# Two transformer blocks on one core: the norms' per-token factors are worked out in PSUM, and those of q and kv are issued between the convolution's last two products

## The chip, the cores and the metric

The kernel runs on one core of a Trainium2 chip, in one launch. A core has five engines that work side by side, each through its own queue in order: PE (TensorE, matrix products and transposes into PSUM), DVE (VectorE), ACT (ScalarE), POOL (GpSimd) and SP, which here only issues transfers. [...] The time of a run is device microseconds from the first to the last instruction and what lies around them; a kernel is told by the median of its runs.

## The reference, cut to what matters

Two blocks work on a sequence of 512 tokens of width 1024. The first has a mixer of latent attention beside a gated causal convolution of width 31, a feed-forward net and a gate; the second another mixer, two squared-ReLU nets and a sparse attention. Norms stand ahead of nearly every part. The stage that the change moves work in is this one:

```python
def rms_norm(x, g):
    xf = x.astype(jnp.float32)
    y = xf * lax.rsqrt(jnp.mean(xf * xf, axis=-1, keepdims=True) + NORM_EPS)
    return (y * g.astype(jnp.float32)).astype(x.dtype)

    proj = xn @ w_in
    q_a, kv_a, k_rope, conv_in = jnp.split(proj, [o1, o2, o3], axis=-1)
    q = (rms_norm(q_a, g_q_a) @ w_q_b).reshape(...)
    kv = (rms_norm(kv_a, g_kv_a) @ w_kv_b).reshape(...)
    ...
    a, gate = jnp.split(conv_in, 2, axis=-1)
    c = a * jax.nn.sigmoid(gate)
    c = causal_depthwise_conv(c, conv_w, conv_b)
```

`q_a` is 384 wide, `kv_a` 256, `a` and `gate` 512 each; the first `rms_norm` of the block is applied late, as a factor per token.

## The kernel before

All activations stand transposed, 128 features by 512 tokens a tile. A product in fp32 is three products of split operands (high by high, high by low, low by high, lines 305 to 307), so each weight and each activation is split: ACT writes the high part (`whi`, line 280), DVE the rest (`wlo`, line 281). Raw weights land in two buffers `raw`, so the transfer of a weight unit waits until the `wlo` of the unit two before it has been made.

A norm needs one factor per token. `SumSq.add` squares the tiles and adds them up; `SumSq.rstd` lets PE sum over the features by products with a column of ones into four columns of a PSUM bank `t`, then works on 128x4 numbers: a scaled mean square `mv` in SBUF (line 439; with a factor `scale` lines 442 to 444), POOL's power of -1/2 into `y` (line 446), and one Newton step on DVE (lines 448 to 452, with a scale 454) that ends in `r`. There are 17 such calls, four of them with a scale: those of kv and of q, whose scale is the block's first norm factor `r1`, and two later. `row_tile` then has PE transpose the broadcast factor (line 462, `t<-ident,r`), and ACT copy it to SBUF as `R` (line 467).

The first mixer computes the convolution's four channel tiles in `conv_in(c)`: two weight units, gate product `pg` and value product `pa`, a sigmoid between, the padded tile `cp`. Each tile has 30 further taps: of even tiles ACT scales (`tap`, line 604) and POOL adds (`cy`, line 605), of odd tiles DVE does both (line 607). The tiles 0 to 2 come first, then kv's two units and `w_kr`, q's three units, and `conv_in(3)`. After that stands the copy of the rotated keys (`kr` by `rep`, line 674), then kv's `sk.rstd(r1)` and its rows `Fk`, q's `sq_.rstd(r1)` and its rows `Fq`. Next is the value product (lines 697 to 699), whose PSUM banks belong to a new phase of the pool: the first waits until ACT has read the last rows out of their bank. Line 765 makes the first key tile `kf`, with which the attention starts; it wants all 30 additions of tile 2 only after its last head.

The order on each engine is not written out by hand: the program is handed to a scheduler that simulates it and emits each engine's queue by its own estimate, with the taps at a high priority. A small edit therefore moves instructions in many places.

Of the kernel before, what the change touches and what calls it, by code (L numbers as in the profile page):

```python
# [7 lines left out]
FT = mybir.dt.float32  # L8
FR = mybir.dt.float32r
I32 = mybir.dt.int32  # L10
OP = mybir.AluOpType
# [11 lines left out]
EPS = 1e-6  # L23
# [191 lines left out]
def _body(tc, A, out):  # L215
    nc = tc.nc
    V, S, P, G = nc.vector, nc.scalar, nc.tensor, nc.gpsimd
# [3 lines left out]
    sp = tc.alloc_tile_pool(name="sp", bufs=2, reuse_waits="tile")  # L221
# [23 lines left out]
    def bank(tag):  # L245
        return ps[0].tile([128, T], FT, name=tag, bufs=banks[tag])
# [12 lines left out]
    def col(name, i):  # L259
        c = _COL0[name] + i  # L260
        return cols[:, c:c + 1]
# [3 lines left out]
    def unit(src, gain=None, eng=V, pl=None, size=1024, bufs=(2, 2), dst=None, chunks=1):  # L265

        n = src.shape[-1]
        pl = pl or wp
        raw = pl.tile([128, size], FT, name="raw", bufs=bufs[0])[:, :n]
        for i in range(chunks):  # L270
            a = slice(i * n // chunks, (i + 1) * n // chunks)
            nc.sync.dma_start(raw[:, a], src[:, a])
        if gain is not None:
            r3 = raw.rearrange("p (k c) -> p k c", k=KT)
            c0 = _COL0[gain]
            G.tensor_tensor(r3, r3, cols[:, c0:c0 + KT, None].to_broadcast([128, KT, n // KT]), op=OP.mult)
        hi, lo = dst or (pl.tile([128, size], FR, name=w, bufs=bufs[1])[:, :n] for w in ("whi", "wlo"))
        for i in range(chunks):
            a = slice(i * n // chunks, (i + 1) * n // chunks)
            S.copy(hi[:, a], raw[:, a])  # L280
            eng.tensor_tensor(lo[:, a], raw[:, a], hi[:, a], op=OP.subtract)  # L281
        return hi, lo

    def split(src, h, l, scale=None, eng=None):
        if scale is None:
            S.copy(h, src)  # L286
            (eng or V).tensor_tensor(l, src, h, op=OP.subtract)  # L287
        else:
            S.activation(h, src, AF.Copy, scale=scale)
            V.scalar_tensor_tensor(l, src, scale, h, op0=OP.mult, op1=OP.subtract)  # L290
        return h, l

    def split_in(pl, tag, src, scale=None, bufs=None, eng=None):
        h = pl.tile([128, T], FR, name=tag + "h", bufs=bufs)
        l = pl.tile([128, T], FR, name=tag + "l", bufs=bufs)
        return split(src, h, l, scale, eng)

    def mm(acc, u, acts, m=128, c0=0, cols_=128, first=True, last=True, ts=None):
        hi, lo = u
        n = len(acts)  # L300
        if ts is not None:
            acc, acts = acc[:, ts], [(h[:, ts], l[:, ts]) for h, l in acts]
        for k, (h, l) in enumerate(acts):
            s = slice(k * cols_ + c0, k * cols_ + c0 + m)
            P.matmul(acc, hi[:, s], h, start=first and k == 0, stop=False)  # L305
            P.matmul(acc, hi[:, s], l, start=False, stop=False)  # L306
            P.matmul(acc, lo[:, s], h, start=False, stop=last and k == n - 1)  # L307
# [6 lines left out]
    def gemm(src, acts, u=None, tag="mm"):  # L314
        acc = bank(tag)
        mm(acc, u or unit(src), acts)
        return acc
# [84 lines left out]
    class SumSq:  # L402
# [25 lines left out]
        def rstd(self, scale=None, ts=ALL):  # L428

            p = bank("t")  # L430
            b0, n = ts.start // 128, (ts.stop - ts.start) // 128
            for i in range(n):
                b = b0 + i
                tiles = [self.sum] if self.whole else [self.sum, self.last[b // 2]]
                for j, a in enumerate(tiles):
                    P.matmul(p[:, i:i + 1], a[:, b * 128:(b + 1) * 128], ones, start=j == 0, stop=a is tiles[-1])
            mv = sp.tile([128, 4], FT, name="mv")[:, :n]
            if scale is None:
                V.tensor_scalar(mv, p[:, :n], 1.0 / (128 * self.n), EPS, op0=OP.mult, op1=OP.add)
            else:  # L440
                scale = scale[:, b0:b0 + n]
                V.scalar_tensor_tensor(mv, p[:, :n], 1.0 / (128 * self.n), scale, op0=OP.mult, op1=OP.mult)
                V.tensor_tensor(mv, mv, scale, op=OP.mult)
                V.tensor_scalar(mv, mv, EPS, None, op0=OP.add)
            y = sp.tile([128, 4], FT, name="y")[:, :n]
            G.tensor_tensor(y, mv, mhalf[:, :n], op=OP.pow)
            a = sp.tile([128, 4], FT, name="a")[:, :n]
            V.tensor_tensor(a, mv, y, op=OP.mult)
            V.tensor_tensor(a, a, y, op=OP.mult)
            V.tensor_scalar(a, a, -0.5, 1.5, op0=OP.mult, op1=OP.add)  # L450
            r = sp.tile([128, 4], FT, name="r", bufs=4)[:, :n]
            V.tensor_tensor(r, y, a, op=OP.mult)
            if scale is not None:
                V.tensor_tensor(r, r, scale, op=OP.mult)
            return r

    def rows(c, p=None, ts=ALL):
# [7 lines left out]
    def row_tile(c, square=False):  # L465
        r = sp.tile([128, T], FT, name="R", bufs=2)
        S.activation(r, rows(c), AF.Square if square else AF.Copy)
        return r
# [8 lines left out]
    def tmp():  # L477
        return scratch("tmp")
# [110 lines left out]
    r1 = s1.rstd()  # L589
# [17 lines left out]
                    V.scalar_tensor_tensor(conv_y[c] if k == CW - 2 else conv_acc[c], cp[c][:, k:k + T], w,  # L607
                                           conv_acc[c], op0=OP.mult, op1=OP.add)

    def conv_in(c):  # L610
        pg = gemm(A["w_in"][2 * c], xg, first.pop(0) if first else None)
        pa = gemm(A["w_in"][2 * c + 1], xg, first.pop(0) if first else None)
        gt = tmp()
        V.tensor_tensor(gt, pg, R1, op=OP.mult)
        S.activation(gt, gt, AF.Sigmoid)
        V.tensor_tensor(gt, gt, R1, op=OP.mult)
        V.tensor_tensor(cp[c][:, CW - 1:], pa, gt, op=OP.mult)
        conv_y[c] = mx.tile([128, T], FT, name=f"cy{c}")
        if c % 2:
            conv_acc[c] = cyp.tile([128, T], FT, name="cy")  # L620
        S.activation(conv_acc[c] if c % 2 else conv_y[c], cp[c][:, CW - 1:], AF.Identity, bias=col("conv_b", c),
                     scale=col("conv_w", c * CW + CW - 1))

    for c in range(3):
        conv_in(c)
        conv_taps(c)
# [14 lines left out]
    n = xgp.tile([64, T], FT, name="rn")  # L641
# [14 lines left out]
    sk = SumSq(2)  # L656
# [10 lines left out]
    sq_ = SumSq(3)  # L667
    for c in range(3):
        acc = gemm(A["w_in"][10 + c], xg)
        sq_.add(acc)  # L670
        split(acc, *qa[c], col("g_q_a", c))
    conv_in(3)
    prep = bank("mm")
    P.matmul(prep, rep, kt_, start=True, stop=True)
    krr = split_in(mx, "krr", prep)
    ck = sk.rstd(r1)
    Fk = row_tile(ck)
    cq = sq_.rstd(r1)
    Fq = row_tile(cq)
    for par in range(2):  # L680
        V.scalar_tensor_tensor(rope[par], rope[par], -rope_sc, Fq, op0=OP.mult, op1=OP.mult)
# [78 lines left out]
    for hp in range(MH // 2):  # L760
# [5 lines left out]
        for par in range(2):  # L766
            a = slice(0, 64) if par == 0 else slice(64, 128)
# [62 lines left out]
    for ts, ms in zip(HALVES, ((4, 5, 6, 7), (6, 7, 4, 5))):  # L830
# [4 lines left out]
        r = sm.rstd(ts=ts)  # L835
# [51 lines left out]
    for ch in range(3):  # L887
        hid = []
        for f in range(8 * ch, min(8 * ch + 8, FT1)):
# [4 lines left out]
            y = tmp()  # L894
            S.activation(y, gpad[:, 2:], AF.Copy, scale=col("ffn_dw_w", 3 * f + 2))
            for k in range(2):
                V.scalar_tensor_tensor(y, gpad[:, k:k + T], col("ffn_dw_w", 3 * f + k), y,
                                       op0=OP.mult, op1=OP.add)
# [17 lines left out]
    for ts, ms in zip(HALVES, (range(3, 8), (6, 7, *range(3, 6)))):  # L916
# [4 lines left out]
        r = sd.rstd(r2, ts)  # L921
# [56 lines left out]
    for c in range(KT):  # L978
# [8 lines left out]
        y = tmp()  # L987
        S.activation(y, gpad[:, 2:], AF.Copy, scale=col("a_conv_w", 3 * c + 2))
        for k in range(2):
            V.scalar_tensor_tensor(y, gpad[:, k:k + T], col("a_conv_w", 3 * c + k), y,  # L990
                                   op0=OP.mult, op1=OP.add)
# [271 lines left out]
    for j in range(4):  # L1263
        a = slice(32 * j, 32 * j + 32)
# [161 lines left out]
```

## Time and profile before

| what | value |
|---|---|
| median of 3 runs | 1960.42 us (1957.62 to 1962.92) |
| profiled execution | 1962.15 us, of which the span is 1959.9 us |
| PE busy | 1873.8 us, 96% |
| DVE, ACT, POOL busy | 67%, 49%, 21% |
| mean granted TensorE clock | 0.98 |
| longest wait of PE | 12.5 us, at 96 to 108 us |

A line of the timeline reads: start, duration, engine, line, operation, output from inputs, shapes, a count, and in brackets how long the engine had been idle and what released it. In the chain of waits each piece is what the next one waited for. A busy PE overlaps its instructions, so matmuls that start 0.23 us apart are shown 0.39 us long.

### The profile page before, as it was taken

Reading aid. Unit: us, or ns where it says so; the run is one execution under the profiler, and the core shown is the slowest. Engines: PE = TensorE matmul, PEld = TensorE weight load, DVE = VectorE, ACT = ScalarE, POOL = GpSimd, SP = SyncE. Lnnn points to the kernel's source line nnn. Section 1 sums busy time; section 2 is a strip of 40 time slices with the busy share of each in tenths; the row PEclk is TensorE's granted clock in tenths of the full one; section 3 lists DMA queues with packets and bytes.
Section 4 is the critical chain, followed back from the end, with each engine's and each line's share of the span. In section 5 each row is a group of like instructions: output and inputs, shape, how many; then the busy total and the mean of one; then the engine's idle time right before and its main releaser. Section 6 shows DMA issues by size and latency. Waiting matters only on the chain.

```text
span 1959.9 us, 27632 instructions
## 1 busy us (share of the span) xinstructions
PE 1873.8 (96%) x10198; PEld 1591.5 (81%) x10198; DVE 1303.7 (67%) x2277; ACT 957.1 (49%) x1755; POOL 410.7 (21%) x397
## 2 busy tenths in 40 slices
PE   8979989999999999999999999889999989999996
PEld 6757878888888878878889888778888878889895
DVE  7878476245355864486666576869887977666654
ACT  6676544333234432254444444646656765444443
POOL 2884240000002310010000002336454420000001
PEclk9989999999999999999999999999999989999998
DMA  4221322333222222334544542354332134554532
GB/s 148 83 58 41 95 82 91 92 97 97 93 88 89 87 86 89 110 103 127 141 125 129 148 128 75 102 155 128 78 89 79 36 100 130 149 131 130 149 94 75
DMA packets 82742, 202.11 MB, mean 103 GB/s; under 512 B 9904, under 2 KB 18288, under 8 KB 82608
## 3 DMA queue, kind: packets, MB, share of 16 engines
q1 hardware_dynamic: 77744, 184.88, 31.1%
q0 software_dynamic: 4032, 14.68, 4.4%
q8 instruction: 80, 1.31, 0.3%
q10 hardware_dynamic: 832, 0.79, 0.1%
q14 instruction: 54, 0.44, 0.1%
HBM read 187.73 MB, written 2.10 MB: 97 GB/s over the span
## 4 chain that ended last, share of the span: by engine, by line
PE 77%; DVE 11%; ACT 3%; DMA 3%; POOL 2%; issue 2%; SPq 0%; DVEq 0%; POOLq 0%; ACTq 0%
PE mm L305 18%; PE mm L306 18%; PE mm L307 18%; PE y L372 3%; PE y L370 3%; PE y L371 3%; PE mm L372 2%; PE mm L371 2%; PE mm L370 2%; POOL cy L605 2%; DVE wlo L281 1%; PE s L497 1%; PE o L530 1%; PE t L522 1%; DVE pw L503 1%
## 5 line engine op out<-in xcount | busy, mean ns | idle before, releaser
L280 ACT CAST whi<-raw 128x512 fp32r<-128x512 f32 (+4 forms) x342 | 260.8, 769 | 460.8 <-PE mm L306 336.7
L281 DVE TENSOR_TENSOR wlo<-raw,whi 128x512 fp32r<-128x512 f32 (+4 forms) x318 | 300.1, 949 | 116.2 <-ACT whi L280 112.4
L306 PE MATMUL mm<-hidl,whi 128*128 128x512 f32 (+1 forms) x794 | 302.1, 381 | 0.1
L305 PE MATMUL mm<-hidh,whi 128*128 128x512 f32 (+1 forms) x794 | 296.9, 381 | 5.1 <-ACT hidh L286 5.0
L307 PE MATMUL mm<-hidh,wlo 128*128 128x512 f32 (+1 forms) x794 | 298.8, 380 | 0.6 <-DVE wlo L281 0.6
L306 PE MATMUL mm<-xgl,whi 128*128 128x512 f32 (+1 forms) x608 | 234.1, 386 | 2.7 <-DVE xgl L290 2.7
L307 PE MATMUL mm<-xgh,wlo 128*128 128x512 f32 (+1 forms) x608 | 233.9, 386 | 0.0
L305 PE MATMUL mm<-xgh,whi 128*128 128x512 f32 (+1 forms) x608 | 232.9, 386 | 0.7 <-ACT whi L280 0.7
L305 PEld LDWEIGHTS mm<-hidh,whi 128*128 128x128 f32 x794 | 149.7, 189 | 32.8 <-ACT hidh L286 5.7
L307 PEld LDWEIGHTS mm<-hidh,wlo 128*128 128x128 f32 x794 | 150.1, 189 | 28.8 <-DVE wlo L281 0.8
L306 PEld LDWEIGHTS mm<-hidl,whi 128*128 128x128 f32 x794 | 150.4, 190 | 27.9 <-DVE hidl L287 0.9
L344 POOL DMA_DIRECT2D raw<-mlp1f x28 | 24.6, 879 | 552.6 <-DVE wlo L281 257.8
L306 PEld LDWEIGHTS mm<-xgl,whi 128*128 128x128 f32 x608 | 115.2, 190 | 28.8 <-DVE xgl L290 3.8
L305 PEld LDWEIGHTS mm<-xgh,whi 128*128 128x128 f32 x608 | 115.1, 190 | 26.3 <-ACT whi L280 1.5
L307 PEld LDWEIGHTS mm<-xgh,wlo 128*128 128x128 f32 x608 | 115.4, 190 | 24.6
L287 DVE TENSOR_TENSOR wlo<-raw,whi 128x1024 fp32r<-128x1024 f32 x56 | 68.5, 1223 | 87.8 <-ACT whi L286 87.6
L421 POOL TENSOR_TENSOR ssq<-ssq,sq 128x512 f32<-128x512 f32 (+1 forms) x58 | 71.5, 1234 | 255.9 <-ACT sq L418 254.9
L505 ACT ACTIVATE pw<-pw,nm 128x512 f32<-128x512 f32 (+3 forms) x160 | 89.4, 560 | 48.3 <-DVE nm L503 47.2
L286 ACT CAST whi<-raw 128x1024 fp32r<-128x1024 f32 x56 | 58.7, 1050 | 99.1 <-DMA raw<-mlp1f 83.3
L1034 DVE TENSOR_TENSOR x<-mm,x 128x512 f32<-128x512 f32 x116 | 79.5, 686 | 36.1 <-PE mm L307 36.1
L605 POOL TENSOR_TENSOR cy<-cy,tap 128x512 f32<-128x512 f32 x60 | 87.2, 1454 | 22.5 <-ACT tap L604 19.0
L287 DVE TENSOR_TENSOR hidl<-tmp,hidh 128x512 fp32r<-128x512 f32 x94 | 64.3, 685 | 7.3 <-ACT hidh L286 7.3
(866 smaller groups left out, 4667.4 us busy)
## 6 DMA issues: line engine op xcount, KB each, us to landing
raw<-mlp SPq DMA_DIRECT2D x140, 256.0 KB, 2.8
raw<-mlp1f SPq DMA_DIRECT2D x56, 512.0 KB, 3.7
raw<-mlp1f POOLq DMA_DIRECT2D x28, 512.0 KB, 6.8
raw<-a_in SPq DMA_DIRECT2D x24, 512.0 KB, 3.5
raw<-w_gate SPq DMA_DIRECT2D x22, 512.0 KB, 3.6
raw<-w_up SPq DMA_DIRECT2D x22, 512.0 KB, 3.5
raw<-w_down SPq DMA_DIRECT2D x16, 512.0 KB, 3.5
zraw<-mlp1f SPq DMA_DIRECT2D x28, 256.0 KB, 3.6
```

What stands on the lines that cost most here:

```text
L280: S.copy(hi[:, a], raw[:, a])
L281: eng.tensor_tensor(lo[:, a], raw[:, a], hi[:, a], op=OP.subtract)
L287: (eng or V).tensor_tensor(l, src, h, op=OP.subtract)
L305: P.matmul(acc, hi[:, s], h, start=first and k == 0, stop=False)
L306: P.matmul(acc, hi[:, s], l, start=False, stop=False)
L307: P.matmul(acc, lo[:, s], h, start=False, stop=last and k == n - 1)
L370: P.matmul(acc, hi[:, s], h, start=first and j == 0, stop=False, skip_group_check=True)
L371: P.matmul(acc, hi[:, s], l, start=False, stop=False, skip_group_check=True)
L372: P.matmul(acc, lo[:, s], h, start=False, stop=j == 3, skip_group_check=True)
L505: S.activation(t, t, AF.Exp, bias=nm[:, i:i + 1], scale=-1.0, accum_out=rs[:, i:i + 1])
L605: G.tensor_tensor(conv_y[c], conv_y[c], t, op=OP.add)
L1034: V.tensor_tensor(x[m], acc, x[m], op=OP.add)
```

## The change

`rstd` keeps the mean square and the Newton step's products in spare columns 8 to 8+n of the PSUM bank that holds the sums. POOL's power still reads SBUF, so one copy of `m` into `mv` is added per call; the tile `a` is gone. And `conv_in` takes a function that is called between its two products: for tile 3 it issues the factors of kv and q, whose rows stay behind the `kr` product.

```diff
@@ SumSq.rstd
-            mv = sp.tile([128, 4], FT, name="mv")[:, :n]
+            m = p[:, 8:8 + n]
             if scale is None:
-                V.tensor_scalar(mv, p[:, :n], 1.0 / (128 * self.n), EPS, op0=OP.mult, op1=OP.add)
+                V.tensor_scalar(m, p[:, :n], 1.0 / (128 * self.n), EPS, op0=OP.mult, op1=OP.add)
             else:
                 scale = scale[:, b0:b0 + n]
-                V.scalar_tensor_tensor(mv, p[:, :n], 1.0 / (128 * self.n), scale, op0=OP.mult, op1=OP.mult)
-                V.tensor_tensor(mv, mv, scale, op=OP.mult)
-                V.tensor_scalar(mv, mv, EPS, None, op0=OP.add)
+                V.scalar_tensor_tensor(m, p[:, :n], 1.0 / (128 * self.n), scale, op0=OP.mult, op1=OP.mult)
+                V.tensor_tensor(m, m, scale, op=OP.mult)
+                V.tensor_scalar(m, m, EPS, None, op0=OP.add)
+            mv = sp.tile([128, 4], FT, name="mv")[:, :n]
+            V.tensor_copy(mv, m)
             y = sp.tile([128, 4], FT, name="y")[:, :n]
             G.tensor_tensor(y, mv, mhalf[:, :n], op=OP.pow)
-            a = sp.tile([128, 4], FT, name="a")[:, :n]
-            V.tensor_tensor(a, mv, y, op=OP.mult)
-            V.tensor_tensor(a, a, y, op=OP.mult)
-            V.tensor_scalar(a, a, -0.5, 1.5, op0=OP.mult, op1=OP.add)
+            V.tensor_tensor(m, m, y, op=OP.mult)
+            V.tensor_tensor(m, m, y, op=OP.mult)
+            V.tensor_scalar(m, m, -0.5, 1.5, op0=OP.mult, op1=OP.add)
             r = sp.tile([128, 4], FT, name="r", bufs=4)[:, :n]
-            V.tensor_tensor(r, y, a, op=OP.mult)
-            if scale is not None:
-                V.tensor_tensor(r, r, scale, op=OP.mult)
+            if scale is None:
+                V.tensor_tensor(r, m, y, op=OP.mult)
+            else:
+                V.tensor_tensor(m, m, y, op=OP.mult)
+                V.tensor_tensor(r, m, scale, op=OP.mult)
@@ conv_in
-    def conv_in(c):
+    def conv_in(c, between=None):
         pg = gemm(A["w_in"][2 * c], xg, first.pop(0) if first else None)
+        if between:
+            between()
         pa = gemm(A["w_in"][2 * c + 1], xg, first.pop(0) if first else None)
@@ the first mixer
-    conv_in(3)
+    cs_ = []
+    conv_in(3, lambda: cs_.extend([sk.rstd(r1), sq_.rstd(r1)]))
+    ck, cq = cs_
     prep = bank("mm")
     P.matmul(prep, rep, kt_, start=True, stop=True)
     krr = split_in(mx, "krr", prep)
-    ck = sk.rstd(r1)
     Fk = row_tile(ck)
-    cq = sq_.rstd(r1)
     Fq = row_tile(cq)
```

On PE, before, the end of `conv_in(3)` reads thus: the last products of `pa`, the last of kv's four transposes, q's eight sums over the features, its transposes, the value product (`whi,kva0h`).

```order
356 L307 MATMUL mm<-xg7h,wlo 128x512
357 L462 MATMUL t<-ident,r 128x128
358 L436 MATMUL t<-ones,ssq 128x1
359 L436 MATMUL t<-ones,sq 128x1
360 L436 MATMUL t<-ones,ssq 128x1
361 L436 MATMUL t<-ones,sq 128x1
362 L436 MATMUL t<-ones,ssq 128x1
363 L436 MATMUL t<-ones,sq 128x1
364 L436 MATMUL t<-ones,ssq 128x1
365 L436 MATMUL t<-ones,sq 128x1
366 L462 MATMUL t<-ident,r 128x128 x4
367 L697 MATMUL mm<-whi,kva0h 128x512
```

In the changed kernel the same place on PE is this, and q's eight sums stand behind the first two of `pa`'s 24 products.

```order
359 L305 MATMUL mm<-xg7h,whi 128x512
360 L306 MATMUL mm<-xg7l,whi 128x512
361 L307 MATMUL mm<-xg7h,wlo 128x512
362 L681 MATMUL mm<-kr,rep 128x512
363 L465 MATMUL t<-ident,r 128x128 x8
364 L702 MATMUL mm<-whi,kva0h 128x512
```

So the sums are made inside `pa`, and all eight transposes, of kv's and of q's factors, stand after it.

On DVE, before, q's factors are made at the end of this stretch; `wlo 128x1024` is that of the unit `w_vb`, `cp_106` the padded tile 3.

```order
85 L281 TENSOR_TENSOR wlo<-raw,whi 128x1024
86 L616 TENSOR_TENSOR tmp<-tmp,R 128x512
87 L287 TENSOR_TENSOR krrl<-mm,krrh 128x512
88 L617 TENSOR_TENSOR cp_106<-mm,tmp 128x512
89 L281 TENSOR_TENSOR wlo<-raw,whi 128x384
90 L442 SCALAR_TENSOR_TENSOR mv<-t,r 128x4
91 L281 TENSOR_TENSOR ukbl<-raw,ukbh 128x1024
92 L443 TENSOR_TENSOR mv<-mv,r 128x4
93 L444 TENSOR_SCALAR mv<-mv 128x4
94 L448 TENSOR_TENSOR a<-mv,y 128x4
95 L449 TENSOR_TENSOR a<-a,y 128x4
```

On DVE in the changed kernel the factors stand right behind that `wlo`, and `cp_106`, the unit of 384 columns, `krrl` and `ukbl` behind them.

```order
88 L281 TENSOR_TENSOR wlo<-raw,whi 128x1024
89 L442 SCALAR_TENSOR_TENSOR t<-t,r 128x4
90 L621 TENSOR_TENSOR tmp<-tmp,R 128x512
91 L443 TENSOR_TENSOR t<-t,r 128x4
92 L444 TENSOR_SCALAR t<-t 128x4
93 L446 COPY mv<-t 128x4
94 L449 TENSOR_TENSOR t<-t,y 128x4
95 L450 TENSOR_TENSOR t<-t,y 128x4
96 L451 TENSOR_SCALAR t<-t 128x4
97 L456 TENSOR_TENSOR t<-t,y 128x4
98 L457 TENSOR_TENSOR r<-t,r 128x4
99 L622 TENSOR_TENSOR cp_106<-mm,tmp 128x512
```

On ACT in the changed kernel the two copies of the rows, `R`, stand behind work that before was spread around them (before, the first stood behind `ukbh` and the second four instructions later, behind `cy` and three taps).

```order
94 L607 ACTIVATE tap_562<-cp2_105,cols_72 128x512
95 L626 ACTIVATE cy_972<-cp3_106,cols_72 128x512
96 L286 CAST krrh_976<-mm_974 128x512
97 L280 CAST ukbh_1004<-raw_1006 128x1024
98 L607 ACTIVATE tap_565<-cp2_105,cols_72 128x512
99 L470 ACTIVATE R_980<-t_981 128x512
100 L470 ACTIVATE R_987<-t_988 128x512
```

On POOL q's power stands behind five additions of tile 2 (`cy_539`) instead of eight and a memset; 21 additions of that tile stand ahead of the first key part `kl` on POOL, 23 before.

## Rows read from the trace of the kernel before

**Rows 1.** The page: busy us, share of the span, instructions.

```profile
PE 1873.8 (96%) x10198; PEld 1591.5 (81%) x10198; DVE 1303.7 (67%) x2277; ACT 957.1 (49%) x1755; POOL 410.7 (21%) x397
```

**Rows 2.** Waits of PE: total us, times, longest us.

```profile
PE t L462 <- DVE r L454: 12.5, 1, 12.5
```

**Rows 3.** Timeline of PE around the end of the convolution's products.

```profile
95.59 0.36 PE L436 MATMUL t<-ones,sq 128*128 128x1 f32 x2
...
108.47 1.09 PE L462 MATMUL t<-ident,r 128*128 128x128 f32 x4 [12.52 <-DVE r L454]
110.25 0.79 PE L697 MATMUL mm<-whi,kva0h 128*128 128x512 f32 x1 [0.69 <-ACT R L467]
```

**Rows 4.** The chain of waits there: start, duration, piece.

```profile
86.46 1.22 DVE wlo L281
87.70 4.32 DMA raw<-w_vb
92.12 1.05 ACT whi L280
...
107.21 1.12 DVE r L454
...
109.60 0.61 ACT R L467
```

**Rows 5.** Timeline of DVE, 82 to 121 us.

```profile
82.51 1.26 DVE L448 TENSOR_TENSOR a<-mv,y 128x4 f32<-128x4 f32 x1 [0.25 <-POOL y L446]
...
85.39 1.15 DVE L454 TENSOR_TENSOR r<-r 128x4 f32<-128x4 f32 x1
...
94.35 1.76 DVE L616 TENSOR_TENSOR tmp<-tmp,R 128x512 f32<-128x512 f32 x1
...
96.63 0.67 DVE L617 TENSOR_TENSOR cp<-mm,tmp 128x512 f32<-128x512 f32 x1
...
120.00 0.69 DVE L765 TENSOR_TENSOR kf<-mm,R 128x512 f32<-128x512 f32 x1 [8.48 <-PE mm L307]
```

**Rows 6.** All instructions of four lines: min/median/max ns.

```profile
L442 DVE SCALAR_TENSOR_TENSOR mv<-t,r x4: 146/149/160, 77.5 to 639.4; 128x4 f32<-128x4 f32 x2, 128x2 f32<-128x2 f32 x2
...
L446 POOL TENSOR_TENSOR y<-mv,mhalf x17: 697/1017/1957, 25.1 to 1949.3; 128x4 f32<-128x4 f32 x9, 128x2 f32<-128x2 f32 x8
...
L448 DVE TENSOR_TENSOR a<-mv,y x17: 148/163/1258, 26.5 to 1951.6; 128x4 f32<-128x4 f32 x9, 128x2 f32<-128x2 f32 x8
...
L450 DVE TENSOR_SCALAR a<-a x17: 153/169/2036, 27.4 to 1952.5; 128x4 f32<-128x4 f32 x9, 128x2 f32<-128x2 f32 x8
```

**Rows 7.** Timeline of ACT, 99 to 102 us.

```profile
99.64 1.04 ACT L280 CAST ukbh<-raw 128x1024 fp32r<-128x1024 f32 x1
...
101.07 0.77 ACT L621 ACTIVATE cy<-cp,cols 128x512 f32<-128x512 f32 x1
```

**Rows 8.** Timeline of POOL, 94 to 155 us.

```profile
110.95 11.51 POOL L605 TENSOR_TENSOR cy<-cy,tap 128x512 f32<-128x512 f32 x8 [2.64 <-ACT tap L604]
...
153.54 1.39 POOL L605 TENSOR_TENSOR cy<-cy,tap 128x512 f32<-128x512 f32 x1
```

**Rows 9.** By stretch: its length, then busy us of PE, PEld, DVE, ACT, POOL, clock.

```profile
110.00:115.00 5.00, 4.75 (x11) 3.79 (x12) 1.30 (x2) 3.50 (x7) 3.90 (x3) 0.50 0.00 0
115.00:120.00 5.00, 5.00 (x21) 3.70 (x21) 0.00 (x0) 4.58 (x11) 4.69 (x5) 0.97 0.00 0
...
140.00:160.00 20.00, 18.59 (x97) 14.15 (x96) 20.00 (x45) 14.12 (x38) 15.77 (x15) 1.00 0.19 51
...
255.00:260.00 5.00, 1.71 (x11) 1.34 (x10) 4.24 (x4) 1.11 (x2) 3.72 (x2) 0.87 0.34 116
```

**Rows 10.** Timeline of DVE at the norm after the first mixer.

```profile
256.95 2.29 DVE L452 TENSOR_TENSOR r<-y,a 128x2 f32<-128x2 f32 x1
```

**Rows 11.** Timeline of PE at the norm near 1230 us.

```profile
1233.32 0.39 PE L307 MATMUL mm<-xg0h,wlo 128*128 128x256 f32 x1 [1.60 <-DVE wlo L281]
```

**Rows 12.** Timeline of PE at the last norm.

```profile
1953.02 0.66 PE L462 MATMUL t<-ident,r 128*128 128x128 f32 x2 [3.46 <-DVE r L452]
```

## The prediction, on record before the run

> **What bounds the kernel now.** I read the page first, then PE's waits, then the timeline of PE at the longest of them, then the chain of waits, and last the other engines around it. PE is busy 96% of the span [rows 1], so an edit to the norms can only pay where PE stands still for a norm. The list of PE's waits has one place that stands out: 12.5 us, once, transposes that wait for `r` of line 454 [rows 2]. The timeline places it: the last sums over q's features start at 95.59, the four transposes of q's factors at 108.47, and the value product at 110.25, 0.69 us behind the copy `R` on ACT [rows 3]. The reader is to see that nothing fills that hole: all that follows on PE needs the PSUM phase that the rows `R` end.
>
> The chain of waits says what the 12.5 us are made of [rows 4]. It runs from the `wlo` of the last `w_in` unit (86.46, which frees a raw buffer) to the transfer of `w_vb` (87.70, 4.32 us), its cast (92.12), POOL's additions, and ends in `r` (107.21) and `R` (109.60). So q's factors are late for two reasons: on DVE they stand behind the `wlo` of `w_vb`, `L616`, `L617` and another `wlo`; and the small operations are stretched. A 128x4 operation has a median of 0.16 us, and single ones take 1.26 or 2.04 us [rows 6]: kv's five from `L448` at 82.51 to the end of `L454` at 86.54 take 4.03 us [rows 5].
>
> **The change part by part.**
>
> The form of the factors. The short operations now have at most one operand in SBUF, and all but the copy and `r` write PSUM. The trace has no operation of DVE that writes PSUM. The nearest row below is `L442`, which reads PSUM and one SBUF operand: 0.146 to 0.160 us in all four cases. The nearest above are the stretched ones, 1.26 and 2.04 us [rows 6]. I take 0.16 us, since `L442` has the nearest operands, and 0.20 us from one start to the next. The new copy `mv` is one more of them: 0.2 us on the path, 17 times, which I count only where PE waits.
> [...]
>
> kv's chain. Five operations at 0.2 us instead of 4.03 us put kv's `r` 3.0 us earlier, at 83.5. The `wlo` of the last `w_in` unit, next on DVE, starts there instead of at 86.46, and the SP queue, in which `w_vb` waits for that buffer, issues at 84.8 instead of 87.70. With the same 4.32 us and the same cast the `wlo` of `w_vb` ends near 91.4.
>
> q's chain. The sums over q's features now stand inside `pa`; their inputs are ready, and PE spends on them what it spent before. DVE: `L442` at 91.4, then `L616`'s product (1.76 us before [rows 5]), three short ones and the copy, near 93.7. POOL: `y` stands behind five additions of tile 2. Three of them come ahead of the cast of `w_vb` in both kernels; two more of 1.4 us (eight took 11.51 us [rows 8]) follow the taps that ACT makes behind that cast, and end near 94.2. `y` takes 1.0 us [rows 6], five DVE operations follow, and q's `r` is there at 96.5 instead of 108.3. PE's work ahead ends near 95.5 (it was 95.95, the four transposes of kv within), so it idles 1 us; the eight transposes are done by 98.
>
> What is late next. `R` on ACT stands behind `cy` of tile 3, `krrh`, `ukbh` and a tap. `cy` needs `cp_106` (`L617`, 0.67 us [rows 5]), which on DVE now stands behind q's chain: 97.2. Then `cy` 0.77, a cast of its size 0.6, `ukbh` 1.04 [rows 7], a tap 0.7 and `R` 0.61: the first rows are out at 100.9, and PE's value product starts there instead of at 110.25. `kf` follows at the same distance as before, 9.75 us [rows 3, 5], near 110.7. Term: **-9.3**, between -3.3 (the rival on the form, below) and -12.3 (the rival on the clock).
>
> The attention behind it gives some back. DVE is busy for 20.00 of 20 us there, POOL for 15.77 [rows 9], and POOL's last addition of tile 2 starts at 153.54. POOL's own pace sets these additions: it wins the 2.64 us in which it waited for taps behind `R`, the rest runs at 1.4 us each [rows 8]. With `kf` 9.3 us earlier some (9.3 - 2.6) / 1.4, about five, more additions fall beside the attention; by the order, two more stand behind the first `kl` on POOL. Two at 1.4 us each in POOL's queue would be 2.8; five that each hold DVE for a whole addition 7; none 0. I take **+2.2**, nearest to the two that the order shows.
>
> The other norms. At 253 to 260 the transposes now stand in front of some 20 products of half width (by 5 us for 21 full ones [rows 9], 0.12 us each: 2.4 us of cover gone), and `r`, which took 2.29 us [rows 10], comes 2.1 us earlier: **+0.5**, between -2.1 and +2.4. Near 1230 an `L450` took the 2.04 us of [rows 6], and PE waits 1.60 us for the `wlo` behind it [rows 11]: **-1.5**, between 0 and -1.6. At the end PE waits 3.46 us for the last `r` [rows 12]; on DVE the products of the first half now stand ahead of the second half's factors, not in the midst of them, and ACT gets to its last work sooner. That is between half the wait lost and most of it won; I take half won, **-1.7**. At the rest of the 17 calls other products on PE cover the factors, so their copy costs 0; without that cover it is 0.2 us each, under 3 us.
>
> Sum: -9.3 + 2.2 + 0.5 - 1.5 - 1.7 = -9.8. Against the profiled execution of 1962.15 that is 1952.4; the median of the runs of before is 1.73 lower, and the same difference gives 1960.42 - 9.8 = **1950.6**.
>
> **The rivals.**
> PE keeps its clock (0.14). [...]
> The attention swallows it (0.24). If each of the five additions holds DVE for its whole length the term is 7.2 and not 2.2, and the other norms give nothing: 1960.42 - 9.3 + 7.2 = 1958.3. For it: DVE has no idle time there, and an earlier start changes none of its work. Against: additions that end sooner leave the rest of the attention clear of them, and most of DVE's work there reads PSUM.
> The form changes nothing (0.05): operations in PSUM are stretched like those in SBUF. Then kv's chain keeps its 3 us and q's keeps another 3: -3.3 + 2.2 + 0.5 - 1.7 = -2.3, 1958.1.
> Slower (0.05): a bank `t`, one of two, is now held until the last factor is made, some 2.3 us longer at each call (a power of 1.0 us, six short operations, what `y` waits on POOL). Where a third user of `t` stands at the head of PE's queue, PE waits. It decides from 1.1 us at each of the 15 other calls: 16.5 - 9.8 = +6.7, 1967.1. Against it: the next user of `t` is most often the transpose that needs that same `r`.
>
> **How the numbers follow.** My forecast, with 1947 to 1954.5 as its own range, has 0.52. A measurement of this kernel tells about 0.3%, 5.9 us, from no change, so faster means under 1954.5: the forecast's case, the kept clock and a little of the attention's case, 0.69. Same is the rest of the attention's and the form's, 0.26; slower 0.05. The range leaves out the slower case, the attention's far end and gains beyond the kept clock: 1944.5 to 1958.5.
>
> **What would show it.** Right: PE's wait for `r` falls from 12.5 us to 1 or 2, with a second wait of 2 or 3 us for `R` behind it; the value product starts at 100 to 102, `kf` at 110 to 111; none of the short operations on PSUM takes over 0.2 us; `w_vb` is issued before 85.5; the last addition of tile 2 starts within 3 us of 153.5, and the first attention ends 6 to 8 us earlier. Wrong: short operations of a microsecond remain; the value product is held past 104, by `y` behind POOL's additions or by the work ahead of `R`; the attention ends where it did; or PE's waits for `t` grow at the other norms.

## The result, and the profile after

| | before | after |
|---|---|---|
| median in the runs that were compared | 1960.91 us (1957.62 to 1962.92) | 1939.02 us (1938.5 to 1943.07) |
| ratio, with its 95% interval | | 0.9894 (0.9875 to 0.9914) |
| span of the profiled execution | 1959.9 us | 1937.2 us |
| PE busy | 1873.8 us, 96% | 1858.0 us, 96% |

The kernel is 21.9 us faster where 9.8 were forecast, and 1939.0 lies outside the range of 1944.5 to 1958.5. The forecast's terms together come out near what was written, in part by luck; a term larger than their sum is missing.

The first of PE's waits in the changed kernel, in the form of [rows 2]: total, times, longest.

```profile
PE t L465 <- DVE r L454: 7.5, 3, 3.7
...
PE mm L702 <- ACT R L470: 3.0, 1, 3.0
...
PE t L465 <- DVE r L457: 2.1, 1, 2.1
```

The 12.5 us of q's `r` (now line 457) have become 2.1 us, and a wait of 3.0 us for the rows `R` follows. The timeline of PE there, against [rows 3]:

```profile
98.39 1.09 PE L465 MATMUL t<-ident,r 128*128 128x128 f32 x4 [2.06 <-DVE r L457]
102.50 0.80 PE L702 MATMUL mm<-whi,kva0h 128*128 128x512 f32 x1 [3.02 <-ACT R L470]
```

The timeline of DVE, against [rows 5]:

```profile
83.05 0.17 DVE L449 TENSOR_TENSOR t<-t,y 128x4 f32<-128x4 f32 x1 [0.48 <-POOL y L448]
...
83.87 0.16 DVE L457 TENSOR_TENSOR r<-t,r 128x4 f32<-128x4 f32 x1
...
92.13 1.64 DVE L621 TENSOR_TENSOR tmp<-tmp,R 128x512 f32<-128x512 f32 x1
...
97.26 0.17 DVE L449 TENSOR_TENSOR t<-t,y 128x4 f32<-128x4 f32 x1 [3.01 <-POOL y L448]
...
112.41 0.69 DVE L770 TENSOR_TENSOR kf<-mm,R 128x512 f32<-128x512 f32 x1 [6.01 <-PE mm L307]
```

All short operations are short, 0.17 us at most. What q's chain waits for is its power on POOL, as the timeline of POOL shows, against [rows 8]:

```profile
82.99 13.26 POOL L608 TENSOR_TENSOR cy<-cy,tap 128x512 f32<-128x512 f32 x8
96.21 1.02 POOL L448 TENSOR_TENSOR y<-mv,mhalf 128x4 f32<-128x4 f32 x1
```

The eight additions ahead of it run back to back at 1.66 us each and end at 96.25; at the 1.4 us each of the prediction they would have ended near 94.2. The value product starts 7.75 us earlier than before, and `kf` 7.6.

That leaves some 14 us. They are not at any wait: from one product to the next PE is faster in the long stretches in which nothing waits. By stretch, columns as in [rows 9], first the kernel before, 420 to 480 us, then the changed kernel:

```profile
420.00:480.00 60.00, 60.00 (x259) 48.27 (x258) 30.41 (x37) 21.61 (x27) 0.50 (x5) 1.00 0.32 97
```

```profile
420.00:480.00 60.00, 60.00 (x263) 49.15 (x262) 31.60 (x38) 21.22 (x27) 0.50 (x5) 1.00 0.31 97
```

Both have PE busy all the time, at a granted clock of 1.00, with much the same work on the other engines, and 259 against 263 products. The starts of consecutive products say it more finely. In the kernel before (`xgh`, `xgl` by a weight unit) they lie 229 and 238 ns apart by turns, in the changed kernel 226, 229 and 232 in turn, in the same loop, on the same operands.

### The profile page after: what moved, and what is told of

It is laid out like the page before. It is cut to its first block, busy times and chain, and to the rows that moved or that the text cites. A ratio compares the mean times of both kernels' runs of the same rounds, so it can differ in the third digit from the quotient of the medians.

```text
span 1937.2 us, 27654 instructions
## 1 busy us (share of the span) xinstructions
PE 1858.0 (96%) x10198; PEld 1585.8 (82%) x10198; DVE 1295.1 (67%) x2294; ACT 956.5 (49%) x1755; POOL 412.0 (21%) x397
## 5 line engine op out<-in xcount | busy, mean ns | idle before, releaser
L307 PE MATMUL mm<-xgh,wlo 128*128 128x512 f32 (+1 forms) x608 | 232.4, 383 | 0.4 <-DVE wlo L281 0.4
```

## The experiments

What changes a product's pace and not its order? The tile `a`, which the change no longer needs, stood in the small pool `sp`, 2 buffers of 32 bytes, ahead of most pools of SBUF. Without it every tile behind it on that side of SBUF (the left; other pools are allocated from the top, the right) stands 64 bytes lower: the `xg` of the feed-forward net and of the second block went from 64 to 0 over a multiple of 256 bytes, their weights in `wp`, ahead of `sp`, stay at 192. The first four runs ask whether that is the missing term. Theory A at first was that a product is faster when its moving operand starts at a multiple of 256 bytes.

**The changed kernel at the old addresses.**

```diff
-            y = sp.tile([128, 4], FT, name="y")[:, :n]
+            y = sp.tile([128, 4], FT, name="y")[:, :n]; sp.tile([128, 4], FT, name="a")
```

> The changed kernel with the tile a of 128x4 allocated again in the norms' helper and never used. Every engine's order is that of the changed kernel; the tiles that stand behind it in SBUF are back at the addresses of the kernel before, 64 bytes higher. Theory A (the tile that the change no longer needs moved the products' operands in SBUF, and PE streams them faster from the new addresses: the 512-column products whose moving operand went from 64 to 0 over a multiple of 256 bytes start every 229.3 ns and not every 232.8, 2345 of them, the 256-column ones every 117.6 and not 119.1, 2960 of them, 8.1 + 4.3 = 12.4 us): 1951 to 1952, and 233 ns again between products of 300 to 600 us. Rival B (PE runs faster because the new order feeds it better or because of its clock): 1939, and 229 ns. Rival C (the address matters only through something else that moved, such as the norm's own tiles): between the two.

Measured 1951.47 us against 1958.86 of before in the same comparison, ratio 0.9955 (0.9937 to 0.9972). The stretch of 420 to 480 us is back at 259 products:

```profile
420.00:480.00 60.00, 60.00 (x259) 48.28 (x258) 30.98 (x39) 22.08 (x28) 0.60 (x6) 1.00 0.32 97
```

So 64 bytes that nothing reads or writes cost 12 us (12.4 by the medians, 12.0 by the two ratios), and without the new addresses the change is worth 7.4 us by the medians, 8.8 by the ratio (5.5 to 12.3 by its interval): the forecast was 9.8.

**The kernel before at the new addresses.**

```diff
-            mv = sp.tile([128, 4], FT, name="mv")[:, :n]
+            ma = sp.tile([128, 8], FT, name="mv"); mv = ma[:, :n]
...
-            a = sp.tile([128, 4], FT, name="a")[:, :n]
+            a = ma[:, 4:4 + n]
```

> The kernel before with a and mv made the two halves of one 128x8 tile, so that the tiles behind them stand 64 bytes lower, as in the changed kernel; nothing else is changed, and every engine's order is that of before. Theory A: 12.4 us less than before, about 1948.5, with the wait of 12.5 us at 96 to 108 us still there and 229 ns between the products of 300 to 600 us. Rival B: 1960 to 1961, 233 ns.

Measured 1947.67, ratio 0.9938 (0.9920 to 0.9955), 11.2 us under before by the medians. The hole in PE is still there, and the stretch has 264 products:

```profile
108.56 1.09 PE L462 MATMUL t<-ident,r 128*128 128x128 f32 x4 [12.62 <-DVE r L454]
```

```profile
420.00:480.00 60.00, 60.00 (x264) 49.23 (x263) 32.33 (x39) 21.74 (x27) 0.50 (x5) 1.00 0.32 97
```

The address is the missing term, shown from both sides; rivals B and C fall. Which operands' addresses, and against what, is still open here.

**The other side of SBUF.** The `hid` of the nets stands at 224 in both kernels, in pools allocated from the top. Unused tiles at the ends of four of these pools move it.

```diff
-    ff.release()
+    ff.tile([128, 56], FT, name="pad"); ff.release()
(the same at three more pools)
```

> The changed kernel with an unused tile of 224 bytes at the end of four pools that are allocated from the top of SBUF, which moves their tiles (hid, the first mixer's xg) from 224 to 0 over a multiple of 256 bytes. Orders as in the changed kernel. Theory A: the 2360 or so 512-column products with that moving operand, 233.2 ns apart in both kernels, come to 229 ns, 8 to 10 us less: 1929 to 1931. Rival B: 1939. If only the step from 64 to 0 mattered (a matter of 128 or 256 bytes and 224 as good or bad as any other): 1939 too.

Measured 1932.77 (1927.43 to 1938.21), ratio 0.9870 (0.9845 to 0.9894): a lower ratio than the changed kernel's 0.9894, though the intervals overlap. The stretch of 980 to 1060 us, the first squared-ReLU net, in the changed kernel and in this one:

```profile
980.00:1060.00 80.00, 80.00 (x505) 71.89 (x504) 51.96 (x81) 36.72 (x63) 3.43 (x4) 1.00 0.53 139
```

```profile
980.00:1060.00 80.00, 80.00 (x512) 72.59 (x511) 56.08 (x88) 39.22 (x68) 2.57 (x3) 1.00 0.50 135
```

**The same with 96 bytes instead of 224.**

> The same with 96 bytes instead of 224: those tiles go from 224 to 128 over a multiple of 256 bytes. If a multiple of 128 bytes is what counts: as with 224 bytes, 1929 to 1931 and 229 ns. If a multiple of 256 counts: 1939 and 233 ns. If 64 were enough, the kernel before, with its operands at 64, would not have been slow, so a gain here speaks for 128.

Measured 1939.47, ratio 0.9895 (0.9878 to 0.9911), as the changed kernel. The 2325 products on `hid` are 232.7 ns apart. 128 bytes do not do.

**One part at a time, at the old addresses.** First the factors in PSUM alone: the changed `rstd` with the unused tile, `conv_in` and the calls as before. Then the calls' place alone: the changed `conv_in` and calls, `rstd` as before.

> The factors worked out in PSUM as in the changed kernel, conv_in and the places of the calls as before, the unused tile a kept so that every tile stands where it stood before. With both parts at these addresses the time was 7.4 us under before (1951.47 against 1958.86). Theory A (both parts shorten the same hole, and the other norms gain from the form alone): q's chain starts near 101, behind ukbl, its operations take 0.16 us, r comes near 104.5 and the value product starts near 106 instead of 110.25, 4 us; with the gain at 1230 and at the end some 5 us in all, 1953 to 1956. Rival B (the hole is only shortened by the place of the calls): the value product at 109 to 110, 1957 to 1959. Rival C (the form alone does it all): the value product at 102 to 103, 1951.

Measured 1951.27, ratio 0.9955 (0.9941 to 0.9968). The value product starts at 105.27. PE's wait, and `kf`:

```profile
104.53 1.09 PE L465 MATMUL t<-ident,r 128*128 128x128 f32 x4 [8.90 <-DVE r L457]
```

```profile
115.31 0.69 DVE L768 TENSOR_TENSOR kf<-mm,R 128x512 f32<-128x512 f32 x1 [5.76 <-PE mm L307]
```

> The calls of kv's and q's factors between the convolution's last two products as in the changed kernel, the factors in SBUF tiles as before, all tiles where they stood before. Theory A: the operations are stretched to 1.1 to 1.3 us beside POOL's additions, q's r comes 3 to 4 us later than with both parts (98.2), near 102, and the value product near 106; nothing is gained at the other norms beside what the order does: 1954 to 1957. Rival B (the place of the calls carries the hole's gain): value product at 102 to 103, 1951 to 1952. Rival C (the place is worth nothing by itself): 110, 1959.

Measured 1949.52, ratio 0.9943 (0.9923 to 0.9964). PE's waits, one of the factors' operations, of which single ones are long again in SBUF, and `kf`:

```profile
102.61 1.09 PE L462 MATMUL t<-ident,r 128*128 128x128 f32 x4 [6.84 <-DVE r L454]
106.49 0.80 PE L699 MATMUL mm<-whi,kva0h 128*128 128x512 f32 x1 [2.80 <-ACT R L467]
```

```profile
99.03 2.02 DVE L450 TENSOR_SCALAR a<-a 128x4 f32<-128x4 f32 x1
```

```profile
116.46 0.69 DVE L767 TENSOR_TENSOR kf<-mm,R 128x512 f32<-128x512 f32 x1 [6.49 <-PE mm L307]
```

In the hole theory A holds: `kf` comes 4.7 us earlier by the form alone, 3.5 by the place alone, 7.9 by both at these addresses (112.11). In the whole time the parts can't be told apart: either alone gives what both give (0.9955, 0.9943 and 0.9955, intervals that overlap). Beyond the hole the three traces differ in ways that are not all the edit's. With the place alone PE wins 3.4 us between its 7050th and 7950th product (1397 to 1561 us), and there every engine's order is that of before: two of PE's waits for DVE, 1.7 and 1.3 us in the trace of before, are not there this time. It wins 3.1 us more at the end, where the order does differ; with both parts PE loses 2.2 us near 263 us. I did not try these orders one by one, and what makes the same order faster in one trace stays open.

**What about the address.** The kernel before with moving operands at 0 on both sides is the sum of the second and the third run's edits:

> The kernel before with a and mv in one 128x8 tile and the unused tiles of 224 bytes at the ends of the four pools at the top: all orders as before, the products' moving operands at a multiple of 256 bytes on both sides. If the address gain is additive (11.2 us for the left side, 6.7 for the right by the medians so far): 1958.9 - 17.9 = 1941, as fast as the changed kernel without its change of the norms. If PE's faster products only run into other engines: 1946 to 1948.

Measured 1941.56, ratio 0.9900 (0.9885 to 0.9915). Layout alone, with the norms untouched, comes within 2.5 us of the whole change. Theory A would be content. But some 150 products of before with both operands at 64 were as fast (229.6 ns apart) as those at 0, so the products were measured by themselves:

```diff
+    for dm in range(0, 64, 8):
+        for dw in range(0, 64, 8):
+            run(dm, dw, 512, 2)   # 24 products: moving operand from column dm on, weights from dw on
```

> Products by themselves: 512-column fp32r products in the kernel's pattern (high by high, high by low, low by high), with the start of the moving operand and that of the weights each set to every multiple of 32 bytes within 256, 24 products each, then 256 columns with two starts of the weights; the rest of the computation is left out. Theory A (the moving operand's start against 256 bytes): 229 ns from start to start where it is a multiple of 256, 233 elsewhere, whatever the weights' start. Theory A2 (it is the two starts against each other, since the kernels' products with both at 64 were 229.7 apart): 229 along the diagonal. Rival D (the pace depends on what the other engines read at the time): one pace for all.

Theory A falls and A2 holds. Mean ns from start to start, past the first few of each 24, by the place within 256 bytes at which each operand starts:

| moving at | weights at 0 | 32 | 64 | 96 | 128 | 160 | 192 | 224 |
|---|---|---|---|---|---|---|---|---|
| 0 | 226.7 | 233.4 | 233.5 | 234.3 | 233.5 | 233.5 | 228.9 | 233.3 |
| 64 | 228.9 | 233.3 | 226.7 | 233.4 | 233.4 | 234.2 | 233.5 | 233.5 |
| 128 | 233.6 | 233.6 | 228.9 | 233.2 | 226.7 | 233.4 | 233.5 | 234.3 |
| 224 | 233.4 | 233.5 | 234.2 | 233.5 | 233.3 | 228.9 | 233.3 | 226.7 |

It is the start of the moving operand less that of the weights, within 256 bytes, that counts: 226.7 ns at 0, 228.9 at 64, 233 to 234 elsewhere, and the four starts not shown say the same within 1 ns (the two that stand out are 227.3 at a difference of 0 and 232.6 at 128). The trace shows it plainly: the first and the last of 24 products, moving operand at 0, with the weights at 0 (difference 0), at 192 (64) and at 128 (128).

```profile
239.77 0.39 PE L236 MATMUL acc<-movh,wth 128*128 128x512 f32 x1
...
244.99 0.40 PE L236 MATMUL acc<-movh,wtl 128*128 128x512 f32 x1
...
228.67 0.40 PE L236 MATMUL acc<-movh,wth 128*128 128x512 f32 x1
...
233.95 0.39 PE L236 MATMUL acc<-movh,wtl 128*128 128x512 f32 x1
...
217.47 0.40 PE L236 MATMUL acc<-movh,wth 128*128 128x512 f32 x1
...
222.84 0.39 PE L236 MATMUL acc<-movh,wtl 128*128 128x512 f32 x1
```

That is 5.22, 5.28 and 5.37 us for 23 steps. No other engine works beside PE here, and the patterns are those of the kernels: 229 and 238 by turns at 128, as before; 226, 229, 232 at 64, as after. The change took the left side's difference from 64 - 192, that is 128, to 0 - 192, that is 64. The two runs on the right side fit as well: by the addresses of the built programs the 224 bytes took the differences there from 224 and 32 to 0 and 64 (233.2 to 229.2 ns), the 96 bytes to 128 and 192 (232.7).

Two more runs put A2 to the test in the kernel. Moving the weights and no moving operand tells it from A:

```diff
-    wp = tc.alloc_tile_pool(name="wp", bufs=2, reuse_waits="tile")
     sp = tc.alloc_tile_pool(name="sp", bufs=2, reuse_waits="tile")
+    wp = tc.alloc_tile_pool(name="wp", bufs=2, reuse_waits="tile")
```

> The kernel before with the small pool sp allocated ahead of the weights' pool wp, not behind it: wp's weights go from 192 to 64 over a multiple of 256 bytes, all moving operands stay where they were (64 and 224), all orders are those of before. Theory A (the moving operand's own start): nothing changes, 1960 to 1961, 233 ns at moving operands that start at 64. Theory A2 (the difference of the two starts within 256 bytes, as the products by themselves showed: 226.7 ns at 0, 228.9 at 64, 233 to 234 elsewhere): the 2240 left-side products of 512 columns go from a difference of 128 to 0 and save 3.7 ns (the 229.3 of the changed kernel's products at 0) to 6.3 ns each, 8 to 14 us; those on the right go from 32 to 160, 0.5 ns worse, 0.6 us; the 256-column ones about 0.5 ns worse, 0.9 us: 1948 to 1954.

Measured 1949.08, ratio 0.9951 (0.9931 to 0.9970), as A2 says and A does not. 2403 products at a difference of 0 are 227.8 ns apart, and the stretch has the most products of all:

```profile
420.00:480.00 60.00, 60.00 (x267) 49.67 (x266) 32.59 (x39) 22.40 (x28) 0.59 (x6) 1.00 0.31 97
```

> The changed kernel with the four unused tiles of 224 bytes and with sp ahead of wp: nearly all products of 512 and 256 columns have a difference of 0 between the two starts. Theory A: as with the four tiles alone, 1932.8, since no moving operand moves. Theory A2 with the kernels' own paces (512 columns 229.3 at 0 as at 64, 256 columns 119.3 at 0 and 116.5 at 64): 2080 x 2.8 ns, 6 us more, 1938 to 1939; with those of the products by themselves (226.7 against 228.9 at 512): 7 us less for these, 1931 to 1933.

Measured 1933.93 (1930.51 to 1934.4), ratio 0.9866 (0.9845 to 0.9887): no better than the four tiles alone, just above the lower of the two estimates. Its 4677 products of 512 columns are 227.9 ns apart, where 3136 of those tiles' kernel are 229.3; its 3604 of 256 columns 119.4, where 2000 of the other are 116.7. What the wide products win the narrow ones lose, which the last run looks at by itself:

> The products by themselves with 256 and 128 columns: two starts of the moving operand, eight of the weights, 96 products each; the rest of the computation is left out. Theory A2: the pace goes by the difference alone, so both starts give the same eight paces; by the kernels 116 to 117 ns at 64 and 32, 119 at 0 and 128 with 256 columns. Theory A: by the moving operand's start.

With 256 columns and the moving operand at 128 the paces at differences 0, 32, 64, ... 224 are 120.0, 117.8, 117.8, 120.0, 120.0, 117.3, 117.8 and 118.3 ns; at 192 they are the same but for three (118.7 at 128, 120.0 at 160, 113.3 at 192). The run of products before it had 256 columns too, at eight starts of the moving operand: there as well 64 gives 117.8 and 0 gives 119.7, and a second pair with a difference of 192, moving operand at 64 and weights at 128, takes 113.3. So with 256 columns 64 is better than 0, and the difference is not all of it: two pairs at 192 take 113.3 and a third (128 and 192) 117.8. With 128 columns all sixteen pairs are at 111.7.

## Why the prediction was wrong, step by step

**The step that failed** is in the count of the parts of the change: "the form of the factors" was costed by its operations alone, and that the tile `a` is gone stood in the description of the change as if it cost nothing. It moved the operands of 2186 products of 512 columns from 232.98 to 229.32 ns and of 1725 of 256 columns from 118.83 to 116.37: 2186 x 3.66 + 1725 x 2.46 ns = 8.0 + 4.2 = 12.2 us. The runs give 12.4 (1951.47 less 1939.02) and 11.2 (1958.86 less 1947.67), by the ratios 12.0 and 12.1. I had no rival for it either, since all of them spoke of waits or of the clock, and of the signs that I named none looks at the pace of the products: most of them came true beside a time outside the range. It could have been seen blind: the built program has each tile's address, and within the trace of before products at four differences could be set side by side.

**The sum of -9.8** was right within what the runs can tell, but in part by luck. The changed kernel at the old addresses gains 7.4 us by the medians and 8.8 by the ratio; its trace, by which the terms can be read, has a span of 1950.4 us against 1959.9, 9.5 us less. Term by term, by the starts of products of the same number in these two traces and, in the hole, by `kf`:

| step | forecast | measured at the old addresses |
|---|---|---|
| hole between the convolution and the attention (`kf`) | -9.3 | -7.9 |
| attention gives back, up to 181 us | +2.2 | +0.6 |
| norm at 253 to 260 us | +0.5 | +0.1 |
| behind that norm, 263 to 284 us | 0 | +2.3 |
| norm near 1230 us | -1.5 | -1.6 |
| last net, 1912 to 1934 us | 0 | -2.3 |
| last norm | -1.7 | -2.1 |
| elsewhere (the rest to -9.5) | 0 | +1.4 |

The terms that I had named come out within 1.6 us each. The luck is in two that I had not, +2.3 and -2.3, which cancel. The second is no work or wait that the change took away. From 1610 to 1917 us every engine's order is that of before, and PE has the same wait of 2.50 us for `hidh` at 1912; behind it the granted clock fell to 0.50 in the trace of before and stayed at 1.00 in that of the changed kernel at the old addresses. The stretch behind the wait, in this order:

```profile
1915.00:1920.00 5.00, 5.00 (x12) 3.90 (x13) 2.97 (x6) 2.88 (x6) 0.11 (x1) 0.50 0.00 0
```

```profile
1910.00:1915.00 5.00, 5.00 (x23) 3.94 (x22) 3.17 (x6) 3.77 (x8) 1.36 (x2) 1.00 0.24 71
```

In the eleven traces of the two kernels and their variants that wait is 2.50 us each time; the clock stayed at 1.00 in five of them and fell in six.

The form: right. None of the operations on PSUM exceeds 0.171 us in the changed kernel, against 1.258 and 2.036 of [rows 6]:

```profile
L450 DVE TENSOR_TENSOR t<-t,y x17: 154/168/171, 27.5 to 1929.3; 128x4 f32<-128x4 f32 x9, 128x2 f32<-128x2 f32 x8
```

The prediction says that the trace of before has no operation of DVE that writes PSUM; that is wrong. The taps of the odd tiles, line 607, write a PSUM bank in 58 of their 60 products, beside POOL's additions, and none takes over 0.756 us against a median of 0.747. The rival in which the form changes nothing could have been dropped on this row:

```profile
L607 DVE SCALAR_TENSOR_TENSOR cy<-cp,cols,cy x60: 729/747/756, 38.5 to 179.8; 128x512 f32<-128x512 f32 x60
```

With a source in PSUM and at most one in SBUF none of these operations was stretched beside the same additions on POOL. Nor does the source in PSUM show in their length: the median is 168 ns here, against medians of 163 and 169 for the short operations in SBUF [rows 6].

The hole: the mechanism was right, the size 1.4 us off. kv's `r` is there at 84.0 (83.5 forecast) and `w_vb` is issued at 85.4 (84.8); then `y` of q waits for POOL's additions until 96.21 (94.2), eight at 1.66 us where I had reckoned with 1.4, and all behind it is late by as much. The second wait, 3.0 us for `R`, is the one that was forecast.

The clock: the rival in which PE keeps it falls. With two gaps of 2 and 3 us in place of one of 12.5 the granted clock still fell, to 0.50 at 100 to 105 us, as it had at 110 to 115 before [rows 9]. So no run shows the 3.0 us by which that rival put the far end of the hole's term at -12.3; with the changed kernel's orders `kf` came 7.6 and 7.9 us earlier. The stretch in the changed kernel:

```profile
100.00:105.00 5.00, 2.50 (x6) 2.04 (x7) 4.53 (x5) 4.26 (x7) 4.73 (x4) 0.50 0.49 142
```

The attention: it gave back less than forecast, though 9 and not 7 additions of tile 2 stand behind the first `kl` on POOL and the last starts at 154.80, 1.3 us after that of [rows 8]; DVE is at 20.00 of 20 us in both. Rival two, the attention swallowing the gain, falls.

The norm at 253 us: right in size. The cover that is gone cost about what the shorter `r` gave. The transposes, now ahead of the products, wait 3.45 us at the old addresses (3.08 in the changed kernel itself), against 0.90 and 2.39 us in two places before.

```profile
249.41 0.66 PE L465 MATMUL t<-ident,r 128*128 128x128 f32 x2 [3.45 <-DVE r L454]
```

`r` itself is short now, 0.153 to 0.163 us, but the factors stand in DVE's queue among splits of weights and activations; in the changed kernel the copy `mv` stands at 243.11, the first product with `y` at 245.87, and then a split `xgl` of 2.26 us. The form cannot help there. What I had at nothing is lost behind the norm: PE has its products there in another order than before, and at the old addresses it waits twice for `xgl`:

```profile
263.07 0.39 PE L306 MATMUL mm<-xgl,whi 128*128 128x256 f32 x1 [0.79 <-DVE xgl L290]
264.48 0.39 PE L306 MATMUL mm<-xgl,whi 128*128 128x256 f32 x1 [0.80 <-DVE xgl L290]
```

With only the form changed, 2.0 us are lost there too. The changed kernel itself, with the same order, loses 1.4 us in the norm and nothing behind it; why stays open.

The last norm: -2.1 for -1.7, but not by the wait that I halved. The wait for `r` is about as long as in [rows 12], 3.08 us against 3.46. What went is the wait ahead of it, for the sum of squares, 3.51 us before and 1.30 now; ACT gets to the squares sooner, as forecast. From the kernel before, then from the changed kernel at the old addresses:

```profile
1947.71 0.35 PE L436 MATMUL t<-ones,ssq 128*128 128x1 f32 x2 [3.51 <-DVE ssq L421]
```

```profile
1937.84 0.35 PE L436 MATMUL t<-ones,ssq 128*128 128x1 f32 x2 [1.30 <-DVE ssq L421]
...
1943.24 0.66 PE L465 MATMUL t<-ident,r 128*128 128x128 f32 x2 [3.08 <-DVE r L454]
```

Slower, by a bank `t` held longer: no wait for a `t` bank appears among PE's waits.

## What to carry to other kernels

An edit that adds or drops a tile can shift all that is allocated behind it on that side: here one of 128x4 did, by 64 bytes. Before its time is put down to the operations, compare the addresses of the products' operands in the two builds, and repeat the change with an unused tile that keeps them. Where PE is the bound, try the start of the moving operand and that of the weights against each other: here two small tiles merged into one, and a few unused ones added, made the kernel before 1% faster with its orders unchanged. And read each part of a change in the stage in which it acts: in the hole the parts nearly add up (4.7 and 3.5 us against 7.9), while whole times also carry waits and clock levels that differ from one trace to the next under the same order (1.7 and 1.3 us, 0.50 and 1.00).

## What the runs showed of the hardware

A product of fp32r operands (the type in which the split fp32 values are multiplied) with 512 columns started every 226.7, 228.9 or 233 to 234 ns, at a granted clock of 1.0, by the difference of its two operands' starts within 256 bytes of SBUF, with no other engine at work; within the kernels the same products took 227.6 to 229.6 (difference 0, the least with the weights moved), 229.3 (64) and 232.4 to 233.8 ns (128, 160, 192, 224 and 32). With 256 columns the same differences gave 113.3 to 120.0 ns in another order, with 128 columns 111.7 at all of them. What makes it so stays open, and the two pairs of starts at which 256 columns took 113.3 ns were not followed up.

In the changed kernel the short DVE operations of 128x4 on PSUM, with at most one source in SBUF, took at most 0.171 us, beside POOL's additions too; in the run with the place alone, in SBUF, single ones took 1.18 to 2.02 us at the same place. And after the same wait of PE, 2.50 us, the granted clock fell in six traces and not in five.
